# An encoder block on one core: value products of the attention with the values stationary in column halves, and group factors that are formed ahead of the values

## The chip, the cores and the metric

The kernel runs on one core of one Trainium2 chip. The metric is the device time of one execution in microseconds. The core has a tensor engine (PE, with its weight loads listed as PEld), a vector engine (DVE), a scalar engine (ACT), GpSimd (POOL) and a sync engine (SP); each works through its own list of instructions, whose order is fixed when the kernel is built, and waits on semaphores of the others. DMAs are issued by SP, POOL and ACT, and each of these engines issues them in the order of its own list.

## The reference, cut to what matters

One block of a hybrid encoder: a combined input projection, dilated window attention in three groups of four heads, gated linear attention (GLA), a gated merge of both, and an MLP. Sequence 1024, width 1024, all in float32. The part in question is the attention:

```python
outs, lses = [], []
for gi, (win, dil) in enumerate(ATTN_PAIRS):          # (128,1), (512,4), (2048,16)
    ...
    o_g, lse_g = _dilated_group(aq[:, :, hs], ak[:, :, hs], av[:, :, hs], bias, dil, k_side)
    outs.append(o_g)
    lses.append(lse_g)
mix_w = jax.nn.softmax(jnp.stack(lses, axis=0), axis=0)
y_attn = jnp.sum(mix_w[..., None] * jnp.stack(outs, axis=0), axis=0)
...
merged = (jax.nn.sigmoid(gate_a) * (y_attn @ w_attn_branch[l])
          + jax.nn.sigmoid(gate_g) * (y_gla @ w_gla_branch[l]))
```

Within a group, `m` is the maximum of a query's scores, `e = exp(s - m)`, `den = sum(e)`, the output `(e @ v) / den`, and `lse = m + log(den)`. The three groups' outputs of a head slot are so mixed with weights that come from the three pairs of `m` and `den`; the mix equals the sum of the three products `e @ v`, each with a factor per query and head (a share).

## The kernel before, in words

The projections are matmuls of 128x512 (`mm3`, L97, three passes L101 to L103 for each pair of split operands), cut into steps by `proj` (L588). Their results are collected in `cr`, a ring of four, and stored to the DRAM tile `spill` by SP (L621). The attention runs in between: 24 tiles of 128 queries, group g=2 first, then g=1, then g=0, eight tiles each. `att` (L762) makes the parts of a tile, and `visit` (L931) calls, for visit i, the loads of tile i+1, the values of tile i-2, the scores of tile i, the transposes of tile i-1, the blend of tile i-2 and the transposed mix of tile i-3. `units` (L942) spreads the visits over the projection steps. The tile scheduler that builds the program then settles the order on each engine, so that parts of neighbouring steps can trade places.

A tile's way: POOL loads q and k from `spill` (L770) and v from `vdr`; `scores` multiplies them on PE (L803, the two heads of a pair in the two row halves), DVE adds the bias and takes the maximum (L809, statistics in `sm`), ACT takes the exponential (L814); `turned` transposes `e` on PE (L830) and DVE and ACT copy it to `et` (L837). `values` (L844) multiplies: the stationary operand is `et` (128 keys x 128 queries), the moving one 64 columns of v, for each head; the result `avp` lies in one PSUM bank as 128 queries x 256. DVE copies it with the statistics into rows of 264 numbers (L854, L855). For g=2 and g=1 POOL stores those rows to `rows` in natural order; for g=0 POOL loads the rows of the other two groups back into `R` (L821), `weigh` (L878) and `blend` (L887) form factors and the mixed result on DVE and ACT, and `mixed` (L868) transposes it on PE (L872), copies it on ACT into `yat` and stores it to `yadr` by POOL (L874).

After the last projection steps `branches` loads the pieces of the GLA result (`ygdr`) and of the attention result (`yadr`) into `pre` by SP (L963), splits each in two on ACT and DVE (L148, L149) into `yg` and `ya`, and the merge multiplies them (`ps<-ya`, `ps<-yg`). SP's list also holds the branch weights (`raw<-in_wb`, L90) and the gates (`gate<-spill`, L1004).

## Time and profile before

| | |
|---|---|
| median of 3 runs | 1380.88 us (1380.69 to 1384.24) |
| profiled execution | 1383.76 us |
| its span, first to last instruction | 1382.0 us |
| mean granted TensorE clock | 0.997 |
| attention on PE (first scores to last values product) | 306.2 to 567.2 us |
| first merge matmul | 600.71 us |
| SP waiting at the spill stores for DVE's `cr` | 132.1 us |
| POOL waiting for `avp` before it loads v (L784) | 58.4 us |

The profile shows one execution; busy times of instructions overlap within an engine's pipeline, so that the distance between two starts is the price of the first. A row names the engine, the line, the operation and out<-in by the program's names. A DMA's row gives the median time from its issue to its landing.

### The profile page before, as it was taken

What the parts mean: (1) busy time and instruction counts of PE and PEld (TensorE: products, weight loads), DVE (VectorE), ACT (ScalarE), POOL (GpSimd) and SP (SyncE); (2) the same over time, 40 slices, a digit from 0 to 9 for tenths busy, and PEclk for the clock granted to TensorE, in tenths of its full rate; (3) what the DMA queues carried; (4) which work ended last, traced back from release to release, by engine and by line L of the source; (5) the groups of instructions that cost most, each with busy time, mean ns of one, the idle gap of its engine ahead of it and who ended that gap; (6) DMA issues with size and microseconds to landing.
All of it is one profiled execution on the core that took longest, in us unless ns stands there. A gap on an engine that the chain in (4) does not pass through costs nothing.

```text
span 1382.0 us, 19028 instructions
## 1 busy us (share of the span) xinstructions
PE 1370.8 (99%) x6837; PEld 1153.0 (83%) x6837; DVE 1011.3 (73%) x1748; ACT 630.7 (46%) x1207; POOL 99.1 (7%) x153
## 2 busy tenths in 40 slices
PE   9999999999999999999999999999999999999998
PEld 6989998788888888888888888888888888888886
DVE  6377768677565677666667787878867897786988
ACT  5346645334344344354416655555556433333343
POOL 0000100013222232000001000000000000000002
PEclk9999999999999999999999999999999999999998
DMA  7262326575444443465753565666655965445313
GB/s 247 71 190 87 108 71 225 183 206 176 157 145 159 136 143 127 139 225 191 270 213 141 200 221 191 222 208 217 219 205 157 365 220 167 152 131 160 105 31 122
DMA packets 105907, 238.57 MB, mean 173 GB/s; under 512 B 20101, under 2 KB 28805, under 8 KB 105812
## 3 DMA queue, kind: packets, MB, share of 16 engines
q1 hardware_dynamic: 99220, 218.47, 47.4%
q0 software_dynamic: 6304, 18.49, 4.4%
q8 instruction: 54, 0.88, 0.3%
q10 hardware_dynamic: 288, 0.39, 0.1%
q14 instruction: 41, 0.34, 0.1%
HBM read 160.67 MB, written 77.68 MB: 172 GB/s over the span
## 4 chain that ended last, share of the span: by engine, by line
PE 90%; DVE 3%; DMA 2%; issue 2%; ACT 2%; POOL 0%; SPq 0%; POOLq 0%; ACTq 0%; DVEq 0%
PE ps L101 18%; PE ps L102 18%; PE ps L103 18%; PE mm L101 9%; PE mm L102 9%; PE mm L103 9%; PE avp L844 2%; PE tr L830 1%; PE sc L803 1%; ACT xr L1196 1%; DMA xrh<-in_xT 1%; DMA praw<-in_wfm 1%; PE sc L406 0%; PE tr L376 0%; DMA pwhi<-in_wfm 0%
## 5 line engine op out<-in xcount | busy, mean ns | idle before, releaser
L1177 ACT CAST T<-hp 128x1024 fp32r<-128x1024 f32 x36 | 37.8, 1051 | 107.6 <-PE ps L102 68.1
L102 PE MATMUL mm<-wlo,x 128*128 128x272 f32 (+1 forms) x240 | 74.5, 311 | 0.7 <-DVE wlo L94 0.7
L101 PE MATMUL mm<-whi,x 128*128 128x272 f32 (+1 forms) x240 | 75.0, 313 | 0.0
L103 PE MATMUL mm<-whi,x 128*128 128x272 f32 (+1 forms) x240 | 74.6, 311 | 0.0
L814 ACT ACTIVATE e<-e,sm 128x256 f32<-128x256 f32 (+2 forms) x96 | 43.4, 453 | 51.6 <-DVE sm L809 51.6
L102 PE MATMUL ps<-B,B 128*128 128x512 f32 x160 | 62.2, 389 | 0.0
L103 PE MATMUL ps<-B,B 128*128 128x512 f32 x160 | 62.2, 389 | 0.0
L101 PE MATMUL ps<-B,B 128*128 128x512 f32 x160 | 60.9, 390 | 0.5 <-ACT B L1177 0.5
L101 PE MATMUL ps<-T,T 128*128 128x512 f32 x144 | 56.0, 389 | 0.0
L102 PE MATMUL ps<-B,T 128*128 128x512 f32 x144 | 56.0, 389 | 0.0
L102 PE MATMUL ps<-T,T 128*128 128x512 f32 x144 | 56.0, 389 | 0.0
L103 PE MATMUL ps<-B,T 128*128 128x512 f32 x144 | 56.0, 389 | 0.0
L103 PE MATMUL ps<-T,T 128*128 128x512 f32 x144 | 56.0, 389 | 0.0
L101 PE MATMUL ps<-B,T 128*128 128x512 f32 x144 | 56.0, 389 | 0.0
L1578 DVE TENSOR_TENSOR acc<-ps,acc 128x512 f32<-128x512 f32 x68 | 45.8, 690 | 12.8 <-PE ps L103 12.2
L1178 DVE TENSOR_TENSOR T<-hp,T 128x1024 fp32r<-128x1024 f32 x36 | 44.1, 1224 | 14.1 <-ACT T L1177 14.0
L101 PE MATMUL mm<-x,pwlo 128*128 128x512 f32 x128 | 51.1, 399 | 1.4 <-DVE cu L642 1.4
L642 DVE TENSOR_TENSOR cr<-cu,mm 128x512 f32<-128x512 f32 x44 | 35.2, 800 | 23.3 <-PE mm L103 23.0
L1683 POOL TENSOR_TENSOR mv<-mv,mhalf 128x1 f32<-128x1 f32 x8 | 7.0, 880 | 607.3 <-DVE mv L1682 605.8
L103 PE MATMUL mm<-x,pwlo 128*128 128x512 f32 x128 | 50.0, 391 | 0.0
L102 PE MATMUL mm<-x,pwlo 128*128 128x512 f32 x128 | 50.0, 391 | 0.0
L101 PE MATMUL ps<-T,fraw 128*128 128x512 f32 x128 | 49.6, 390 | 0.4 <-ACT T L1177 0.4
(497 smaller groups left out, 4228.8 us busy)
## 6 DMA issues: line engine op xcount, KB each, us to landing
hdr<-c SPq DMA_DIRECT2D x112, 256.0 KB, 2.5
hp<-hdr SPq DMA_DIRECT2D x56, 512.0 KB, 3.6
spill<-cr SPq DMA_DIRECT2D x64, 256.0 KB, 3.0
praw<-in_wfm SPq DMA_DIRECT2D x16, 512.0 KB, 5.0
pwhi<-in_wfm SPq DMA_DIRECT2D x16, 512.0 KB, 4.6
gate<-spill SPq DMA_DIRECT2D x32, 256.0 KB, 3.7
wa<-in_w SPq DMA_DIRECT2D x16, 512.0 KB, 4.5
wb<-in_w SPq DMA_DIRECT2D x16, 512.0 KB, 6.4
```

The lines of the kernel that those rows point to most:

```text
L101: T.matmul(ps, lh, rh, start=first and i == 0, stop=False, skip_group_check=more)
L102: T.matmul(ps, lh, rl, start=False, stop=False, skip_group_check=more)
L103: issued["pe"] = T.matmul(ps, ll, rh, start=False, stop=last and i == n - 1, skip_group_check=more)
L642: issued["add"] = V.tensor_tensor(o, a, b, op=OP.add)
L803: mm = T.matmul(sps[i][:, pr, 0:w], q[ps_, pr], k[ps_, pr, 0:w], start=True, stop=True)
L814: issued["exp"] = A.activation(e, e, AF.Exp, bias=sm[:, h:h + 1], scale=-1.0, accum_out=sm[:, 4 + h:5 + h])
L830: T.transpose(tp[0:hi - lo, pr, j], b["e"][i][:, pr, lo:hi], ident)
L844: return T.matmul(av[:, h * 64:h * 64 + 64], b["et"][h % 2][p0:p0 + vv.shape[0], h // 2, j], vv[:, h * 64:h * 64 + 64], start=j == h == 0, ...
L1177: A.copy(o[:, 0], src)
L1178: V.tensor_tensor(o[:, 1], src, o[:, 0].bitcast(F32), op=OP.subtract)
L1196: A.activation(q[i][:, k], tp[:, k], AF.Identity, bias=cols[:, c + 8:c + 9], scale=cols[:, c:c + 1])
L1578: V.tensor_tensor(m, p, m, op=OP.add)
```

## The change

The value products take v as the stationary operand, 64 columns at a time, and `et` (128 queries) as the moving one. The two heads of a pair write to the two column halves of the array, so that the result `avp` is already transposed: 64i.. partitions for the head's 64 values, two pairs, 128 queries. For g=2 and g=1 DVE copies it once and POOL stores it to `numdr`; the statistics go by themselves, as 8 numbers a query, to `smdr`, and `stats` loads them back for all eight tiles of g=0. For g=0 the factors are formed from the statistics alone in two units behind the scores (`weigh` with ACT's exponential, `shares`), transposed on PE into a third part of the same PSUM tile (`spread`, 12 x 128), copied by ACT to `fT` and stored by ACT to `fdr`. `loadw` reads them back with two SP DMAs into `W`, each line of 128 to 64 partitions; `quarter` loads the products of the other groups into `R` with four SP DMAs, for two tiles at a time. `values` then multiplies and adds on DVE in place in `W`, and POOL stores the result to `yadr` straight from there. The mix's transposes, `yat` and its ACT copies are gone. `W`, `fT` and `avp` are single buffers. The visits lose one round (26 for 27).

```diff
--- before.py
+++ after.py
@@ -110,7 +110,9 @@
     ygdr = dr.tile([4, 128, S], F32, name="ygdr")
     sdr = dr.tile([2, 5, 128, 2, 512], F32, name="sdr")
     yadr = dr.tile([2, 128, S], F32, name="yadr")
-    rows = dr.tile([2, S, 264], F32, name="rows")
+    numdr = dr.tile([2, 2, 128, S], F32, name="numdr")
+    smdr = dr.tile([2, S, 8], F32, name="smdr")
+    fdr = dr.tile([12, S], F32, name="fdr")
...
@@ -745,11 +747,12 @@
     kq_t, kk_t, kv_t = (ring(ap_, [128, 2, n], F32, m, nm) for nm, n, m in (("aq", 128, 3), ("ak", 256, 2), ("av", 256, 3)))
     e_t, et_t = (ring(ap_, [128, 2, 256], F32, m, nm) for nm, m in (("e", 4), ("et", 3)))
     sm_t, f_t = ring(ap_, [128, 8], F32, 3, "sm"), ring(ap_, [128, 5, 4], F32, 2, "f")
-    st_t, R_t = ring(ap_, [128, 264], F32, 2, "st"), ring(ap_, [128, 3, 264], F32, 2, "R")
+    R, W = ap_.tile([128, 2, 2, 256], F32, name="R"), ap_.tile([128, 3, 2, 128], F32, name="W")
+    s12, fT = ap_.tile([128, 8, 2, 8], F32, name="s12"), ap_.tile([12, 128], F32, name="fT")
+    st_t = turns([R[:, 1, i].rearrange("p (b n) -> p b n", b=2) for i in range(2)], 2)
     sc_t = turns([scp.tile([128, 2, 256], F32, tag="sc", name="sc") for _ in range(2)], 2)
     tr_t = turns([trp.tile([128, 2, 256], F32, tag="tr", name="tr") for _ in range(2)], 2)
-    av = avp.tile([128, 256], F32, tag="av", name="avp")
-    yat = ap_.tile([128, 2, 128], F32, name="yat")
+    av = avp.tile([128, 3, 128], F32, tag="av", name="avp")
 
...
@@ -815,10 +818,6 @@
                                                  accum_out=sm[:, 4 + h:5 + h])
 
         def turned():
-            if g == 0:
-                b["R"] = R_t()
-                for i in range(2):
-                    G.dma_start(b["R"][:, 1 + i], rows[i, t * 128:t * 128 + 128])
             b["et"] = []
             nb = len(b["blks"])
             for i in range(2):
@@ -840,9 +839,10 @@
             nb = len(b["blks"])
 
             def part(j, h):
+                i, pr = h % 2, h // 2
                 lo, hi, vv, p0 = b["blks"][j]
-                return T.matmul(av[:, h * 64:h * 64 + 64], b["et"][h % 2][p0:p0 + vv.shape[0], h // 2, j],
-                                vv[:, h * 64:h * 64 + 64], start=j == h == 0, stop=j == nb - 1,
+                return T.matmul(av[64 * i:64 * i + 64, pr], vv[:, h * 64:h * 64 + 64],
+                                b["et"][i][p0:p0 + vv.shape[0], pr, j], start=j == pr == 0, stop=j == nb - 1,
                                 skip_group_check=True)
 
             with tc.issue_after(part(0, 0).ins):
@@ -850,59 +850,82 @@
                     for h in range(4):
                         if j or h:
                             issued["small"] = part(j, h)
-            st = b["R"][:, 0] if g == 0 else st_t()
-            V.tensor_copy(st[:, 0:256], av)
-            V.tensor_copy(st[:, 256:264], b["sm"])
+            if g:
+                st = st_t()
+                V.tensor_copy(st, av[:, 0:2])
+                G.dma_start(numdr[g - 1, :, :, t * 128:t * 128 + 128].rearrange("b p n -> p b n"), st)
+                return
+            V.tensor_tensor(W[:, 0], av[:, 0:2], W[:, 0], op=OP.mult)
+            for i in range(2):
+                c = ORD[i + 1]
+                n = 128 // c
+                num = R[:, i].rearrange("p b (c j) -> p b j c", c=c)[:, :, t % 2 * n:t % 2 * n + n]
+                wn = W[:, i + 1].rearrange("p b (j c) -> p b j c", c=c)
+                for pr in range(2):
+                    V.tensor_tensor(wn[:, pr], num[:, pr], wn[:, pr], op=OP.mult)
+                V.tensor_tensor(W[:, 0], W[:, 0], W[:, i + 1], op=OP.add)
+            G.dma_start(yadr[:, :, t * 128:t * 128 + 128].rearrange("b p n -> p b n"), W[:, 0])
+
+        def weigh():
+            sm = b["sm"]
             if g == 1:
-                G.dma_start(rows[0].rearrange("(u j c) w -> c u j w", u=2, c=4)[t // 2, t % 2], st)
+                G.dma_start(smdr[0].rearrange("(u j c) w -> c u j w", u=2, c=4)[t // 2, t % 2], sm)
             elif g == 2:
-                G.dma_start(rows[1].rearrange("(j r) w -> r j w", r=8)[t], st)
+                G.dma_start(smdr[1].rearrange("(j r) w -> r j w", r=8)[t], sm)
             else:
-                b["f"] = weigh(b["R"])
-
-        def mix():
+                o = s12[:, t]
+                b["f"] = f = f_t()
...
+                A.activation(f[:, 0:3], f[:, 0:3], AF.Exp)
+
+        def shares():
             if g == 0:
-                b["o"] = o = st_t()[:, 0:256]
-                blend(b["R"], b["f"], o)
-
-        def mixed():
+                f, den, o = b["f"], b["sm"][:, 4:8], s12[:, t, :, 4:8]
+                V.tensor_tensor(den, den, f[:, 0], op=OP.mult)
+                V.tensor_tensor(o, o, f[:, 1:3], op=OP.mult)
+                V.tensor_tensor(f[:, 4], den, o[:, 0], op=OP.add)
+                V.tensor_tensor(f[:, 4], f[:, 4], o[:, 1], op=OP.add)
+                V.reciprocal(f[:, 4], f[:, 4])
+                V.tensor_tensor(f[:, 0:3], f[:, 0:3], f[:, 4:5].to_broadcast([128, 3, 4]), op=OP.mult)
+
+        def spread():
             if g == 0:
-                tp = tr_t()
-                for pr in range(2):
-                    T.transpose(tp[:, pr, 0:128], b["o"][:, pr * 128:pr * 128 + 128], ident)
-                A.copy(yat, tp[:, :, 0:128])
-                G.dma_start(yadr[:, :, t * 128:t * 128 + 128].rearrange("b p n -> p b n"), yat)
-
-        return load, scores, turned, values, mixed, mix
-
-    def weigh(R):
-        nm = R[:, :, 256:260]
-        f = f_t()
-        V.tensor_tensor(f[:, 3], nm[:, 0], nm[:, 1], op=OP.min)
-        V.tensor_tensor(f[:, 3], f[:, 3], nm[:, 2], op=OP.min)
-        V.tensor_tensor(f[:, 0:3], f[:, 3:4].to_broadcast([128, 3, 4]), nm, op=OP.subtract)
-        A.activation(f[:, 0:3], f[:, 0:3], AF.Exp)
-        return f
-
-    def blend(R, f, o):
-        den = R[:, :, 260:264]
-        V.tensor_tensor(den, den, f[:, 0:3], op=OP.mult)
-        V.tensor_tensor(f[:, 4], den[:, 0], den[:, 1], op=OP.add)
-        V.tensor_tensor(f[:, 4], f[:, 4], den[:, 2], op=OP.add)
-        V.reciprocal(f[:, 4], f[:, 4])
-        V.tensor_tensor(f[:, 0:3], f[:, 0:3], f[:, 4:5].to_broadcast([128, 3, 4]), op=OP.mult)
-        for g in range(3):
-            num = R[:, g, 0:256].rearrange("p (h d) -> p h d", h=4)
-            V.tensor_tensor(num, num, f[:, g].unsqueeze(2).to_broadcast([128, 4, 64]), op=OP.mult)
-        V.tensor_tensor(R[:, 0, 0:256], R[:, 0, 0:256], R[:, 1, 0:256], op=OP.add)
-        V.tensor_tensor(o, R[:, 0, 0:256], R[:, 2, 0:256], op=OP.add)
+                T.transpose(av[0:12, 2], b["f"][:, 0:3].rearrange("p g h -> p (g h)"), ident)
+                A.copy(fT, av[0:12, 2])
+                A.dma_start(fdr[:, t * 128:t * 128 + 128], fT)
+
+        def loadw():
+            if g == 0:
+                src = fdr.rearrange("(g b i) n -> i g b n", g=3, b=2)
+                for i in range(2):
+                    one = src[i, :, :, t * 128:t * 128 + 128]
+                    SP.dma_start(W[64 * i:64 * i + 64], one.unsqueeze(0).to_broadcast([64, 3, 2, 128]))
+
+        return load, scores, turned, values, weigh, shares, spread, loadw
+
+    def stats(g):
+        for u in range(2):
+            G.dma_start(s12[:, 4 * u:4 * u + 4, g - 1],
+                        smdr[g - 1, 512 * u:512 * u + 512].rearrange("(t p) w -> p t w", p=128))
+
+    def quarter(n):
+        u, q = n // 2, n % 2
+        for g in (1, 2):
+            c = ORD[g]
+            for pr in range(2):
+                src = numdr[g - 1, pr].rearrange("p (c u q j) -> p u q c j", c=c, u=2, q=2)[:, u, q]
+                dst = R[:, g - 1, pr].rearrange("p (c j) -> p c j", c=c)
+                SP.dma_start(dst, src)
 
     def flat(t):
         return t.rearrange("p a b -> p (a b)")[:, 0:512]
 
 
     gated = ap_.tile([128, 3, 512], F32, tag="strip1", name="gated")
-    gating = (turns([flat(e_t()) for _ in range(4)] + [flat(R_t()) for _ in range(2)], 6),
+    gating = (turns([flat(e_t()) for _ in range(4)] + [R[:, i].rearrange("p b n -> p (b n)") for i in range(2)], 6),
               turns([flat(et_t()) for _ in range(3)] + [gated[:, i] for i in range(3)], 6),
               turns([flat(kv_t()) for _ in range(3)], 3))
 
@@ -930,9 +953,11 @@
 
     def visit(i):
 
-        for n, part in ((i + 1, 0), (i - 2, 3), (i, 1), (i - 1, 2), (i - 2, 5), (i - 3, 4)):
+        for n, part in ((i + 1, 0), (i - 1, 6), (i - 2, 3), (i, 1), (i - 1, 2)):
             if 0 <= n < 24:
                 tiles[n][part]()
+        if i in (12, 16):
+            stats(2 if i == 12 else 1)
 
 
     n0 = len(steps) + 14
@@ -940,8 +965,14 @@
         steps += p["steps"]
     n1 = len(steps) - 7
     units = {}
-    for i in range(27):
-        units.setdefault(n0 + 1 + i * (n1 - n0) // 27, []).append(lambda i=i: visit(i))
+    for i in range(26):
+        n = n0 + 1 + i * (n1 - n0) // 27
+        units.setdefault(n, []).append(lambda i=i: visit(i))
+        for k, part, later in ((i, 4, 1), (i, 5, 2), (i - 1, 7, 1)):
+            if 0 <= k < 24 and (later == 1 or k > 15):
+                units.setdefault(n + later, []).append(lambda k=k, part=part: tiles[k][part]())
+        if i in (17, 19, 21, 23):
+            units[n + 1].append(lambda i=i: quarter((i - 17) // 2))
     for i in range(8):
 
         n = n0 - 18 + i * 3 // 2
```

The three places that follow show the end of the attention in the order of each engine. In the order of PE, ahead of the merge, `L844` is the values product, `L103`, `L101` are projection matmuls (`mm`), `L872` is the transposed mix. Before, the last product and what follows it:

```order
L103 MATMUL mm<-xT_2222,pwhi 128x512
L844 MATMUL avp<-av_2253,et_2259 128x64
L844 MATMUL avp<-av_2253,et_2260 128x64
...
L872 MATMUL tr<-ident,st_2266 128x128 x2
L101 MATMUL mm<-x_91,pwlo 128x512
L102 MATMUL mm<-x_91,pwlo 128x512
L103 MATMUL mm<-x_91,pwlo 128x512
```

Behind it stand 144 projection matmuls and then the first `ps<-ya`. In the changed program, from the last projection matmul on (`L896` is the transposed set of factors, `L829` the transposes of `e`, `ps<-yg` the merge):

```order
L103 MATMUL mm<-x_94,px 128x512
L896 MATMUL avp<-ident,f_2267 12x128
L844 MATMUL avp<-et_2262,av_2254 64x128
L844 MATMUL avp<-et_2260,av_2254 64x128
...
L829 MATMUL tr<-ident,e_2258 128x128 x4
L829 MATMUL tr<-ident,e_2259 128x128 x4
L844 MATMUL avp<-et_2261,av_2255 64x128
L844 MATMUL avp<-et_2262,av_2255 64x128
...
L101 MATMUL ps_5183<-yg_5002,whi 128x512
L101 MATMUL ps_5176<-yg_5002,whi 128x512
```

The products of tiles 22 and 23 have moved behind all projection matmuls, and the merge begins with `yg` in place of `ya`. Between the product of tile 21 and the last projection matmul stand one block of scores, one of transposes and 24 projection matmuls.

SP's list at the same place, before (`pre` are the merge's pieces, `raw` its weights):

```order
L621 DMA spill<-cr_2105 128x512
L963 DMA pre<-ygdr 128x512 x4
L963 DMA pre<-yadr 128x512
L621 DMA spill<-cr_2106 128x512
L963 DMA pre<-yadr 128x512
L621 DMA spill<-cr_2107 128x512
L621 DMA spill<-cr_2108 128x512
L963 DMA pre<-yadr 128x512 x2
L90 DMA raw<-in_wb 128x768
L963 DMA pre<-ygdr 128x512
```

And in the changed program:

```order
L905 DMA W<-fdr 64x6x128 x2
L90 DMA raw<-in_wb 128x768
L623 DMA spill<-cr_2110 128x512
L1035 DMA gate<-spill 128x512 x9
L905 DMA W<-fdr 64x6x128 x2
L994 DMA pre<-ygdr 128x512 x4
L994 DMA pre<-yadr 128x512 x4
L994 DMA pre<-ygdr 128x512 x4
L1035 DMA gate<-spill 128x512
```

The pieces have moved from among the spill stores to behind the last one and behind the factors of the last two tiles; nine gates have moved ahead of them.

DVE's list at the end of the attention, in the changed program (`L865` are the products of the other groups with their factors, `L858` that of the tile itself, `L866` the additions, `L836` the copy of the transposes, `L151` the split of the pieces):

```order
L865 TENSOR_TENSOR W<-R,W 128x128 x4
L858 TENSOR_TENSOR W<-avp,W 128x256
L836 COPY et_2261<-tr 128x512
L866 TENSOR_TENSOR W<-W 128x256 x2
L858 TENSOR_TENSOR W<-avp,W 128x256
L865 TENSOR_TENSOR W<-R,W 128x128 x4
L866 TENSOR_TENSOR W<-W 128x256 x2
L151 TENSOR_TENSOR yg_5002<-pre,yg_5002 128x512 x4
L151 TENSOR_TENSOR ya_4998<-pre,ya_4998 128x512
```

Before, the corresponding rows of the last tile stand among projection work:

```order
L854 COPY R_2269<-avp 128x256
L896 TENSOR_TENSOR R_2269<-R_2269,f_2265 128x256
L897 TENSOR_TENSOR R_2269<-R_2269 128x256
L898 TENSOR_TENSOR st_2267<-R_2269 128x256
L149 TENSOR_TENSOR pwlo<-pwhi,pwlo 128x512
L642 TENSOR_TENSOR cr_2106<-cu_2103,mm 128x512
```

The copy of the transposes that the last product needs now stands behind the multiplication of tile 22, and the splits of the pieces follow the last addition directly.

4 lines of the change are left out of this document (added).

## The prediction

> **What bounds the kernel now.** I read the head of the page first, then the chain that ended last, then the stage that the change touches by windows, and only then single rows.
>
> ```profile
> PE 1370.8 (99%) x6837; PEld 1153.0 (83%) x6837; DVE 1011.3 (73%) x1748; ACT 630.7 (46%) x1207; POOL 99.1 (7%) x153
> PE 90%; DVE 3%; DMA 2%; issue 2%; ACT 2%; POOL 0%; SPq 0%; POOLq 0%; ACTq 0%; DVEq 0%
> 530.00:560.00 30.00, 30.00 (x173) 25.43 (x172) 25.80 (x79) 12.95 (x36) 4.88 (x8) 1.00 0.40 122
> 560.00:575.00 15.00, 15.00 (x77) 12.59 (x76) 6.92 (x13) 4.58 (x9) 1.47 (x2) 1.00 0.38 117
> 575.00:610.00 35.00, 35.00 (x155) 28.83 (x154) 20.19 (x31) 15.19 (x24) 0.72 (x1) 1.00 0.66 220
> ```
>
> TensorE (PE) is busy 99% of the span and holds 90% of the chain. In the windows (columns after the stretch: sum, then PE, PEld, DVE, ACT, POOL) it is full through the end of attention and the start of the merge. So a microsecond of PE work taken out here shortens the kernel, and a microsecond in which PE stands still lengthens it; work of DVE, ACT, POOL or the queues counts only where PE comes to wait for it.
>
> The prices of PE's work come from its timeline (start, busy time, line):
>
> ```profile
> 540.47 0.38 PE L872 MATMUL tr<-ident,st 128*128 128x128 f32 x2
> 540.68 0.78 PE L844 MATMUL avp<-av,et 128*128 128x64 f32 x6
> 541.27 0.48 PE L101 MATMUL mm<-x,pwlo 128*128 128x512 f32 x1
> ...
> 544.12 1.22 PE L844 MATMUL avp<-av,et 128*128 128x64 f32 x10
> 545.27 0.92 PE L803 MATMUL sc<-ak,aq 64*128 64x192 f32 x8
> 546.13 1.09 PE L830 MATMUL tr<-ident,e 128*128 128x128 f32 x8
> 546.98 0.47 PE L103 MATMUL mm<-xT,pwhi 128*128 128x512 f32 x1
> ...
> 565.48 2.03 PE L844 MATMUL avp<-av,et 128*128 128x64 f32 x16
> 567.44 0.44 PE L872 MATMUL tr<-ident,st 128*128 128x128 f32 x2
> 567.64 0.48 PE L101 MATMUL mm<-x,pwlo 128*128 128x512 f32 x1
> ...
> 600.71 0.39 PE L101 MATMUL ps<-ya,whi 128*128 128x512 f32 x1
> ```
>
> I take differences of starts, since busy times overlap. One tile's values product is 16 passes: 10 in 1.15 and 6 in 0.59 us, so 0.109 each. A transpose pass over 128 columns costs 0.85 / 8 = 0.106, or 0.83 ns a column. Eight score passes over 192 columns, whose row halves stand in different halves of the array, take 0.86; one after another at 0.83 ns a column they would take 1.27. So **halves of the array do run at once** in this trace, for rows. Between 567.64 and 600.71 stand the 144 projection matmuls that the old order puts behind the last values product: 33.07 / 144 = 0.23 us each. They cover everything that happens between that product and the merge.
>
> **The change, part by part.**
>
> *Values on PE.* There are 320 passes at L844 (160 products). With 64 stationary columns and 128 moving ones, two heads can share the array. At once: 160 pairs; a pair cannot beat one pass over 128 columns (0.106), so 0.109 and 17.4 us in place of 34.9, **−17.4**. One after another: 320 passes at the same 0.109, so nothing. A middle case is set by the weight loads:
>
> ```profile
> L366 PEld LDWEIGHTS tr<-ident,k x32: 139/141/143, 80.0 to 177.4; 128*128 128x128 f32 x32
> L316 PEld LDWEIGHTS tr<-ident,lr x8: 124/126/128, 54.4 to 58.1; 128*96 128x96 f32 x8
> L830 PEld LDWEIGHTS tr<-ident,e x160: 108/140/198, 312.4 to 557.9; 128*128 128x128 f32 x140, 128*64 128x64 f32 x20
> ```
>
> 128, 96 and 64 columns load in 141, 126 and (the minimum) 108 ns. If only these 33 ns come off a 0.109 load and loads stay serial, a pair takes 0.15 and the product saves 34.9 − 160 × 0.152 = 10.6. I take −17.4, being nearest to the score row, the only one of two halves; the ends are −17.4 and 0.
>
> *A rule weighed.* The 10 value passes ahead of L803 take 1.15, and 10 at 0.106 would be 1.06: 0.09 us stands where the row layout changes, and the sum has it already on both sides. The Trainium skill, "TensorEngine Tiling (Array Packing)", Key Properties, says that changing the tiling mode drains the TensorE, and that tiles work independently. By the first, 24 products and 8 narrow transposes, entered and left, would each meet a drain; by the second the halves run at once, as the score row shows for rows. Rival 4 prices the first from the row.
>
> *Transposes.* 16 passes (L872) go, 0.21 / 2 = 0.105 each; 8 small ones of the factors come. 8 × 0.106 − 16 × 0.105 = −0.8. PE's work: **−18.2**.
>
> *Other engines outside the tail.* DVE's prices are these:
>
> ```profile
> L897 DVE TENSOR_TENSOR R<-R x8: 417/422/427, 486.9 to 568.5; 128x256 f32<-128x256 f32 x8
> L891 DVE TENSOR_TENSOR f<-f,R x8: 159/161/164, 471.0 to 554.7; 128x4 f32<-128x4 f32 x8
> L809 DVE CUSTOM_DVE_ANT_0 e<-sc,strip x96: 270/354/426, 306.9 to 548.3; 128x256 f32<-128x256 f32 x40, 128x128 f32<-128x128 f32 x32, 128x192 f32<-128x192 f32 x24
> L809 DVE DVE_READ_ACCUMULATOR2_ANT sm<- x96: 70/84/93, 307.1 to 548.6; 128x1 f32 x96
> L837 DVE COPY et<-tr x19: 407/684/690, 313.7 to 558.7; 128x512 f32<-128x512 f32 x11, 128x256 f32<-128x256 f32 x8
> ```
>
> A g=0 tile loses a 128x256 copy, three multiplications, two additions and a small copy (6 × 0.42 + 0.16 = 2.7) and gets one multiplication of 128x256, four of 128x128 (between 0.16 and 0.42, I take 0.28), two additions and two small operations (2.7). DVE stays as full as it was, beside PE. POOL stores and loads as many pieces as before, at 7% busy. SP gets 32 more issues, 0.32 us each (row below), 10 us over some 100 us. ACT trades eight copies of 128x256 for eight of 12x128 and eight issues. All of this lies beside PE as long as a g=0 visit is long: the new order has 60 to 84 projection matmuls in one, 14 to 19 us, and a tile's new round trip (DVE 3.7, store 3.1, load 3.2) is 10.0. The spill stores queued behind the loads of W have a ring of four buffers as cover; without it each visit would add up to the 3.1 of a store.
>
> *The tail.* This is the price. In the new order only 24 projection matmuls, one score block and two blocks of transposes stand behind the product of tile 21, and none behind that of tile 23; the merge follows directly, with the GLA pieces first. And pre<-ygdr, which the old order had far ahead, is queued on SP behind the last W<-fdr, which waits for W, a single buffer. Its rows:
>
> ```profile
> yadr<-yat POOLq DMA_DIRECT2D x8, 128.0 KB, 3.1
> pre<-yadr SPq DMA_DIRECT2D x4, 256.0 KB, 3.1
> pre<-ygdr SPq DMA_DIRECT2D x8, 256.0 KB, 4.0
> R<-rows POOLq DMA_DIRECT2D x16, 132.0 KB, 2.5
> aq<-spill POOLq DMA_DIRECT2D x24, 128.0 KB, 3.8
> tdr<-trow SPq DMA_DIRECT2D x12, 256.0 KB, 7.2
> DMA to landing us min/median/max: 2.2/3.1/4.6
> L963 SPq DMA_DIRECT2D pre<-ygdr x8: 319/382/407, 572.0 to 593.8; - x8
> L148 ACT CAST yg<-pre x8: 620/622/627, 582.3 to 600.0; 128x512 fp32r<-128x512 f32 x8
> ```
>
> (The line of minimum, median and maximum is that of the tile yat, so of the store yadr<-yat.) The load of W is not in this trace: 192 KB in 512-byte pieces, lying between R<-rows at 2.5 and aq<-spill at 3.8; a broadcast store, tdr<-trow, took 7.2. I take 3.2, the ends are 2.5 and 7.2. From the end V of tile 21's product:
> - DVE: multiplication 0.42, four score reductions 4 × (0.354 + 0.084), copy of et 0.68, two additions 0.84: V + 3.7.
> - Store of yadr 3.1, load of W for tile 22 3.2: V + 10.0.
> - DVE: 4 × 0.28 + 0.42 + copy 0.68 + 0.84 = 3.1; store 3.1: V + 16.2.
> - SP issues two W (0.64), then pre<-ygdr 4.0, ACT's cast 0.62: first merge matmul at **V + 21.4**.
> - PE's work until then: scores 0.86, transposes 2 × 0.85, 24 × 0.23, two products 2 × 0.87, the small transpose 0.1: 9.9. PE stands still for **11.5**.
> - W for tile 23 lands at 16.2 + 3.2, DVE 2.4, store 3.1, pre<-yadr 3.1, cast 0.62: ya is there at V + 28.6. PE has 10 GLA matmuls, 2.3, until V + 23.7: another **4.9**.
>
> Together +16.4.
>
> *The clock.* The granted clock (second figure from the right but two) falls where PE is left idle at the very end:
>
> ```profile
> 1360.00:1370.00 10.00, 10.00 (x46) 8.28 (x45) 9.05 (x23) 4.54 (x12) 1.84 (x2) 1.00 0.29 107
> 1376.00:1382.00 6.00, 1.22 (x2) 0.50 (x2) 0.84 (x2) 1.17 (x3) 0.00 (x0) 0.50 0.49 176
> ```
>
> It is 1.00 with PE full and 0.50 with PE busy for 1.22 of 6 us. A stall of 11.5 us would find it at half as well, and the matmuls behind it run slower until it is back; how long no row shows. Between nothing and 3 us (half speed through a stretch of 6 us), I take +1. The Trainium skill, "TensorE: Matmul & The Clock Gate", on the HAM clock gate, gives about 3.4 us of sustained work until the full clock is back, by which the loss is an estimated 1.7 per long stall; the fall agrees with the row above, the return is shown by no run here.
>
> *Sum:* −18.2 + 16.4 + 1 = −0.8 on the profiled execution, 1383.76 us (span 1382.0, the rest lies around it): 1383.0. The median of the three runs is 1380.88, 2.9 below it, and the same step from there is **1380**.
>
> **The rivals.**
>
> 1. *The tail is shorter.* If the stores land at their minimum of 2.2 and the loads of W at 2.5, three stores and two loads take 0.9 × 3 + 0.7 × 2 = 4.1 out of the chain, and the sum is −5: 1376; with pre<-yadr at 2.5 too, and no clock loss, 1374. For: the queues are quieter in the tail, with no projection weights left to fetch. Against: gate<-spill loads stand there now, nine just ahead on SP.
> 2. *The column halves do not run at once* (ends slower). No row has two column halves; if the array takes them one after another, −18.2 becomes −0.8 and the stall, with 1.7 us more work on PE ahead of it, 14.7: **+15, 1396**. It makes the kernel slower by over 0.3% from a pair price of about 0.15 on, where the gain is 10.6 and the sum +5. For: only row halves are seen at once. Against: nothing in the score rows depends on which halves they are.
> 3. *W lands late* (ends slower). A load of W as dear as tdr<-trow's 7.2 adds 4.0 twice to the chain; at aq<-spill's 3.8 and stores of 3.8 it is 0.6 × 2 + 0.7 × 3 = 3.3. That gives +3 to +7: 1383 to 1388. For: it reads the same six lines 64 times over. Against: 7.2 was measured when 16 projection weights were in flight.
> 4. *A change of layout costs time every time* (ends slower). 24 products and 8 narrow transposes, entered and left, at the 0.09 us that stands between L844 and L803: 64 × 0.09 = 5.8, sum +5, 1386. Against: a transpose of 64 columns between those of 128 has no longer passes (the median of all 160 is 273 ns, the minimum 272):
>
> ```profile
> L830 PE MATMUL tr<-ident,e x160: 272/273/331, 312.4 to 558.0; 128*128 128x128 f32 x140, 128*64 128x128 f32 x20
> ```
>
> 5. *The change does not do what it says*: PE, not the queue, is late at the merge, and no stall appears. Then the whole −18 stays: 1363. The order on each engine is fixed, so I give this little.
>
> **How the numbers follow.** A time within 0.3%, 4.1 us either way, is about what a measurement of this kernel can tell from no change. Forecast, halves at once and the gain given back in the tail: 0.45, 1377 to 1385. Shorter tail: 0.18, and 0.05 for rival 5, together 0.23 faster. Halves not at once 0.16, W late 0.11, layout changes 0.05: together 0.32 slower. The predicted time is 1380. The range runs from rival 1's lower end to rival 2's time, 1374 to 1396; it leaves out rival 5 and mixtures beyond rival 2.
>
> **What would show it.** Right: L844's passes start in pairs, with some 0.109 a pair; PE full until the last projection matmul; then a gap of about 11 us ahead of the first ps<-yg, ended by pre<-ygdr, and a second of about 5 ahead of ps<-ya, ended by pre<-yadr; SP waiting at the last W<-fdr. Wrong: L844's stretch as long as before (rival 2), a gap below 8 us in all (rivals 1 and 5), PE gaps inside the g=0 visits (the spill ring fails as cover), or W<-fdr landing beyond 4 us (rival 3).

## The result, and the profile after

| kernel | median of four runs, us (lowest to highest) | against before (95% interval) | span of the profiled run, us | clock |
|---|---|---|---|---|
| before | 1380.79 (1379.21 to 1384.24) | | 1382.0 | 0.997 |
| changed | 1418.04 (1413.81 to 1419.26) | 1.0261 (1.0231 to 1.029) | 1417.1 | 0.983 |

The change makes the kernel 37 us slower; the forecast was 1380, the range 1374 to 1396. The profiled execution of the kernel before is one of its longer ones, so the spans differ by 35.1 only. The head of the page and the windows of the changed kernel (stretch: sum, PE, PEld, DVE, ACT, POOL busy with counts; then granted clock, DMA share, GB/s):

```profile
PE 1370.2 (97%) x6829; PEld 1136.3 (80%) x6829; DVE 1008.4 (71%) x1748; ACT 631.8 (45%) x1207; POOL 105.3 (7%) x157
480.00:530.00 50.00, 44.52 (x222) 34.59 (x221) 31.94 (x102) 18.96 (x53) 6.54 (x9) 0.95 0.43 133
530.00:560.00 30.00, 30.00 (x166) 23.86 (x165) 19.44 (x58) 9.60 (x26) 4.85 (x7) 0.96 0.46 144
560.00:575.00 15.00, 11.49 (x63) 8.97 (x61) 7.12 (x23) 5.03 (x13) 0.24 (x1) 1.00 0.40 103
575.00:600.00 25.00, 20.91 (x112) 16.28 (x107) 15.95 (x52) 9.35 (x26) 1.86 (x3) 0.86 0.52 140
600.00:620.00 20.00, 8.09 (x58) 5.96 (x56) 6.10 (x19) 6.10 (x10) 1.47 (x2) 0.77 0.57 177
620.00:640.00 20.00, 7.84 (x20) 5.38 (x21) 6.01 (x14) 6.27 (x11) 0.73 (x1) 0.55 0.53 163
```

PE is no longer full from 480 us on, and the clock is below 1.00 in most of the same stretches. The stalls of PE of more than 0.3 us from there on stand in its timeline (start, busy time, last the idle time ahead and what ended it):

```profile
484.57 0.79 PE L101 MATMUL mm<-xT,pwlo 128*128 128x512 f32 x1 [2.21 <-ACT cr L669]
529.41 0.79 PE L101 MATMUL mm<-xT,pwhi 128*128 128x512 f32 x1 [3.20 <-DVE cr L644]
571.39 0.27 PE L896 MATMUL avp<-ident,f 128*12 128x128 f32 x1 [3.35 <-DVE f L892]
591.18 0.38 PE L896 MATMUL avp<-ident,f 128*12 128x128 f32 x1 [4.09 <-DVE f L892]
604.15 1.09 PE L844 MATMUL avp<-et,av 128*64 128x128 f32 x16 [0.34 <-ACT fT L897]
614.66 2.17 PE L844 MATMUL avp<-et,av 128*64 128x128 f32 x16 [8.40 <-DVE et L836]
631.84 1.47 PE L101 MATMUL ps<-yg,whi 128*128 128x512 f32 x2 [15.01 <-ACT yg L150]
```

The first four, 12.9 us, lie inside the g=0 visits, the last three, 23.8 us, where the merge should begin. Behind most of them is one transfer, as the experiments below show; it stands in the list of DMAs and in the waits of DVE:

```profile
W<-fdr SPq DMA_DIRECT2D x16, 192.0 KB, 7.9
pre<-ygdr SPq DMA_DIRECT2D x8, 256.0 KB, 7.0
DVE W L865 <- DMA W<-fdr: 46.4, 7, 8.1
DVE W L858 <- DMA W<-fdr: 15.2, 1, 15.2
```

The load of W takes 7.9 us, not 3.2, and DVE waits 61.6 us for it. That median rests on the three loads of 16 for which the profile gives a landing; by the semaphore records in the trace all 16 landed after 6.3 to 9.4 us. The clock is at half in four stretches (columns: sum, PE's busy time and count, clock, DMA share, GB/s):

```profile
484.47:487.88 3.41, 3.31 (x8) 0.50 0.22 81
528.85:532.26 3.41, 2.85 (x7) 0.50 0.50 144
590.29:597.12 6.83, 5.94 (x31) 0.50 0.58 118
610.77:638.08 27.31, 8.11 (x29) 0.50 0.58 184
```

The account between the two profiled executions is then: stalls from 260 us on 38.0 in place of 2.2, +35.8; the 320 passes of the value products (summed over the distances of their starts in the trace) 24.7 in place of 36.1, -11.4; transposes 0.5 in place of 1.5, -1.0; the lower clock, half of the 20.21 us that PE was busy in those stretches, an estimated +10.1. The sum is +33.5, and 1417.1 - 1382.0 is 35.1. The rest is not in these rows: a change of layout ahead of each product (e4_swap_alone below) would add some 2.4, and some of the value passes ran at half clock and are counted twice.

### The profile page after: what moved, and what is told of

Its sections match the earlier page's. It is cut to its first block, busy times and chain, and to the rows that moved or that the text cites. A ratio compares the mean times of both kernels' runs of the same rounds, so it can differ in the third digit from the quotient of the medians.

```text
span 1417.1 us, 19085 instructions
## 1 busy us (share of the span) xinstructions
PE 1370.2 (97%) x6829; PEld 1136.3 (80%) x6829; DVE 1008.4 (71%) x1748; ACT 631.8 (45%) x1207; POOL 105.3 (7%) x157
## 4 chain that ended last, share of the span: by engine, by line
PE 54%; DMA 2%; ACT 1%; DVE 0%; issue 0%; SPq 0%; DVEq 0%; ACTq 0%
PE ps L102 18%; PE ps L101 18%; PE ps L103 18%; DMA W<-fdr 1%; ACT xr L1227 1%; DMA yadr<-W 0%; DMA gate<-spill 0%; PE ps L1224 0%; PE ps L1735 0%; PE ps L1731 0%; ACT T L1208 0%; PE avp L844 0%; ACT B L1208 0%; PE sc L806 0%; PE mm L103 0%
## 5 line engine op out<-in xcount | busy, mean ns | idle before, releaser
L101 PE MATMUL mm<-whi,x 128*128 128x272 f32 (+1 forms) x240 | 75.1, 313 | 0.0
L103 PE MATMUL mm<-whi,x 128*128 128x272 f32 (+1 forms) x240 | 74.6, 311 | 0.0
L103 PE MATMUL ps<-B,B 128*128 128x512 f32 x160 | 62.2, 389 | 0.0
L101 PE MATMUL ps<-B,B 128*128 128x512 f32 x160 | 60.9, 390 | 0.5 <-ACT B L1208 0.5
L101 PE MATMUL ps<-T,T 128*128 128x512 f32 x144 | 56.0, 389 | 0.0
L103 PE MATMUL ps<-T,T 128*128 128x512 f32 x144 | 56.0, 389 | 0.0
L101 PE MATMUL ps<-B,T 128*128 128x512 f32 x144 | 56.0, 389 | 0.0
L103 PE MATMUL ps<-B,T 128*128 128x512 f32 x144 | 56.0, 389 | 0.0
L644 DVE TENSOR_TENSOR cr<-cu,mm 128x512 f32<-128x512 f32 x44 | 35.3, 802 | 28.5 <-PE mm L103 27.7
L101 PE MATMUL mm<-x,pwlo 128*128 128x512 f32 x128 | 50.6, 395 | 1.0 <-DVE cu L644 1.0
L101 PE MATMUL mm<-xT,pwhi 128*128 128x512 f32 x120 | 48.1, 401 | 3.2 <-DVE cr L644 3.2
L103 PE MATMUL mm<-x,pwlo 128*128 128x512 f32 x128 | 50.3, 393 | 0.0
```

Source lines behind the costliest of these rows:

```text
L101: T.matmul(ps, lh, rh, start=first and i == 0, stop=False, skip_group_check=more)
L103: issued["pe"] = T.matmul(ps, ll, rh, start=False, stop=last and i == n - 1, skip_group_check=more)
L644: issued["add"] = V.tensor_tensor(o, a, b, op=OP.add)
```

## The experiments

Twelve kernels, grouped by question; times are medians, ratios are those to the kernel before on the same chip.

**W from different lines (e1_own_lines).** A line is here a stretch of DRAM that is read in one piece, 512 bytes for the load of W. On the changed kernel, the load reads other numbers from another DRAM tile:

```diff
-                src = fdr.rearrange("(g b i) n -> i g b n", g=3, b=2)
+                src = spill[24:30].rearrange("(g b) p n -> p g b n", g=3)
                 for i in range(2):
-                    one = src[i, :, :, t * 128:t * 128 + 128]
-                    SP.dma_start(W[64 * i:64 * i + 64], one.unsqueeze(0).to_broadcast([64, 3, 2, 128]))
+                    SP.dma_start(W[64 * i:64 * i + 64], src[64 * i:64 * i + 64, :, :, t * 128:t * 128 + 128])
```

> W is loaded from 64 different lines of another DRAM tile in place of the same line 64 times; pieces (512 bytes), size (192 KB), wait for W and place in SP's list stay, the factors that the output is mixed with are other numbers. Theory 1 (the load of W is dear because it reads the same lines 64 times): the load lands in 3 to 4 us instead of 8, the four stalls of PE inside the g=0 visits (12.9 us) go, the tail's stall falls from 23.7 to about 16, the clock loss falls by some 8: 1418 - 13 - 8 - 8 = about 1389 us (1380 to 1395). Rival (the chain over the single buffer W and the place of the loads in SP's list cost the time, whatever a load takes): over 1410 us.

1386.61 us, ratio 1.0044 (1.0028 to 1.006). The list of its DMAs:

```profile
W<-spill SPq DMA_DIRECT2D x16, 192.0 KB, 3.8
pre<-ygdr SPq DMA_DIRECT2D x8, 256.0 KB, 4.6
```

The same number of pieces of the same size, from 64 different lines, lands in 3.8 us, the pieces of the merge behind it land in 4.6 again, and 31 of the 37 us are gone. No stall is left inside the visits. This is what theory 1 said. By the semaphore records, the 14 loads beside the g=0 tiles landed after 3.4 to 4.3 us; the two of the first tile are issued earlier, in another stretch. The trace's packets show where the time goes: a piece takes 27 ns in the median in both kernels, but in the first 1.5 us from the first piece on 122 to 178 pieces of a tile's two loads begin in the changed kernel, and 529 to 667 here. Two other things have changed with the lines: the load no longer waits for the store of the factors (the first one is issued at 356.5 us in place of 470.1), and its access no longer has a step of zero from one partition to the next. The first is answered by e8a_long_lines below, which keeps the wait; the second isn't told apart from the lines.

**The multiplications held back on DVE (e2_mults_behind).**

```diff
-            V.tensor_tensor(W[:, 0], av[:, 0:2], W[:, 0], op=OP.mult)
+            first = V.tensor_tensor(W[:, 0], av[:, 0:2], W[:, 0], op=OP.mult)
...
-                    V.tensor_tensor(wn[:, pr], num[:, pr], wn[:, pr], op=OP.mult)
+                    with tc.issue_after(first.ins):
+                        V.tensor_tensor(wn[:, pr], num[:, pr], wn[:, pr], op=OP.mult)
```

> The changed kernel with the four multiplications R x W of a tile held back until its own product with W is issued, so that DVE reaches the wait for W later in its list. Theory (DVE stands at the wait for W ahead of projection work that PE waits for): the stalls inside the visits (12.9 us, and some 5 of clock) shrink by more than half, the tail stays: about 1405 us. Rival (PE waits for W whatever DVE's order is): no change, 1418 us.

1409.92 us, 1.0212 (1.0188 to 1.0236): 8 us better, where 13 were expected; with two runs, 1407.19 and 1412.66, its interval just overlaps that of the changed kernel. In the changed kernel DVE's timeline shows the reason for the edit, and that of this run why it gives so little:

```profile
526.81 0.37 DVE L865 TENSOR_TENSOR W<-R,W 128x128 f32<-128x128 f32 x1 [5.22 <-DMA W<-fdr]
...
528.67 0.68 DVE L644 TENSOR_TENSOR cr<-cu,mm 128x512 f32<-128x512 f32 x1
```

```profile
528.06 0.69 DVE L637 TENSOR_TENSOR pwhi<-pwhi 128x512 f32<-128x512 f32 x1 [9.39 <-DMA pwhi<-in_wfm]
528.67 0.68 DVE L644 TENSOR_TENSOR cu<-cu,mm 128x512 f32<-128x512 f32 x1
```

SP's timeline of this run, at the same place:

```profile
514.44 1.28 SPq L906 DMA_DIRECT2D W<-fdr  x2
515.82 0.56 SPq L610 DMA_DIRECT2D pwhi<-in_wfm  x1
```

In the changed kernel DVE stands 5.22 us at the wait for W, and the addition that frees PE's bank (L644) comes behind; PE's stall of 3.20 ends there. With the wait out of the way DVE waits for projection weights instead: they were issued right behind the two loads of W and came 12 us later, where such a load takes 4.9 in the median of that run. So, as far as these rows show, a load of W also holds up what is queued behind it, and DVE's order is only part of the matter. What the edit shows is mixed: the stalls up to the product of tile 21 fall from 12.9 to 7.9 us, those behind it stay (25.1 against 23.8), and the edit also moved the 24 projection matmuls that stood behind that product ahead of it.

**The swap by itself (e4_swap_alone).** On the kernel before:

```diff
-                return T.matmul(av[:, h * 64:h * 64 + 64], b["et"][h % 2][p0:p0 + vv.shape[0], h // 2, j],
-                                vv[:, h * 64:h * 64 + 64], start=j == h == 0, stop=j == nb - 1,
+                i, pr = h % 2, h // 2
+                return T.matmul(av[64 * i:64 * i + 64, pr * 128:pr * 128 + 128], vv[:, h * 64:h * 64 + 64],
+                                b["et"][i][p0:p0 + vv.shape[0], pr, j], start=j == pr == 0, stop=j == nb - 1,
```

> The kernel before with one edit: v is the stationary operand in column halves, everything behind it as before; the result lies transposed where the rest takes it as not transposed, so the mix is of other numbers. Theory (the halves run at once, a pass in the mean 0.077 us instead of 0.113 as the traces of before and after have it): 36.1 - 24.7 = 11.4 us off PE at no cost elsewhere: 1369 us. Rival (the gain is taken back by waits for v or avp): 1376 to 1381 us.

1370.48 us, 0.9928 (0.9913 to 0.9942). PE has no stall between 300 and 600 us; a tile's product and its neighbours in the timeline:

```profile
543.38 0.38 PE L873 MATMUL tr<-ident,st 128*128 128x128 f32 x2
543.69 1.09 PE L845 MATMUL avp<-et,av 128*64 128x128 f32 x16
544.72 0.55 PE L830 MATMUL tr<-ident,e 128*128 128x128 f32 x3
```

The product takes 1.03 us. Eight pairs of 0.109 would be 0.87: 0.16 is the change of the layout on leaving. Two transposes ahead of it take 0.31 to its start, and 0.21 in the kernel before: another 0.10 on entering. 24 products at 0.26 are 6.2 us. The 0.16 is part of the passes' own sum, which is 24.0 us in this run, 12.1 below the kernel before; the 0.10 stands in the rows ahead, and 24 of them, 2.4, come off that gain. What is left, 9.7, is what the medians show: 1380.27 - 1370.48 = 9.8. (The 24.0 are 6.6 above the 17.4 of the prediction, more than 24 x 0.16 = 3.8: some products are split into pieces, and each piece pays.)

**Which halves (e5_same_half, e12_one_half).** The first only orders the heads otherwise, `for h in (0, 2, 1, 3)`. The second:

```diff
-                return T.matmul(av[64 * i:64 * i + 64, pr * 128:pr * 128 + 128], vv[:, h * 64:h * 64 + 64],
+                return T.matmul(av[0:64, h * 128:h * 128 + 128], vv[:, h * 64:h * 64 + 64],
...
-            V.tensor_copy(st[:, 0:256], av)
+            for i in range(2):
+                V.tensor_copy(st[64 * i:64 * i + 64, 0:256], av[0:64, 256 * i:256 * i + 256])
```

> As e4_swap_alone (the kernel before with v stationary in column halves, the mix of other numbers), but the four heads of a block in the order 0, 2, 1, 3, so that most neighbours use the same column half. Theory (a pass runs beside the one ahead of it only if that one is in the other half): of four products in a row only the middle two overlap, three steps of 0.107 a pass in place of two, values up by at least 8 us against e4_swap_alone: 1378 to 1386 us. Rival (the array takes any two 64-column passes together, or the gain comes from shorter weight loads alone): 1369 to 1372 us as e4_swap_alone.

> As e4_swap_alone (the kernel before with v stationary, the mix of other numbers), but all four heads write to the same column half, partitions 0 to 63 of the bank; DVE copies it in two pieces of 64 partitions. Theory 2a (a pass is short because its weight load has 64 columns in place of 128, whichever half it is in): 16 passes still take some 0.9 us and the time is that of e4_swap_alone, 1370 us (1369 to 1374, DVE has 24 more copies of 0.4 us). Theory 2b (two passes overlap only in different halves, as the prediction had it): each pass takes 0.107, values are back at 34 us or more, 1380 us or more.

e5_same_half took 1371.79 us (0.9936, 0.9916 to 0.9955), e12_one_half 1388.59 (1.0056, 1.0039 to 1.0073). Their timelines, a product and the row behind it, of the first and of the second:

```profile
544.79 1.14 PE L845 MATMUL avp<-et,av 128*64 128x128 f32 x16
545.87 0.66 PE L830 MATMUL tr<-ident,e 128*128 128x128 f32 x4
```

```profile
548.95 1.52 PE L845 MATMUL avp<-et,av 128*64 128x128 f32 x12
550.41 0.91 PE L803 MATMUL sc<-ak,aq 64*128 64x192 f32 x7
```

In one half, 12 passes take 1.46 us, 0.109 each and the layout change; over both halves in either order 16 take about 1.05. So **the two column halves do run at once, and the gain of the swap is all of that**: in one half the kernel is slower than before, since the layout changes come on top. The expectation for e5_same_half was wrong: the order of the heads matters by 0.05 us a product, 1.2 in all (the medians differ by 1.3, within their intervals), so PE overlaps passes that are not next to each other in its list. There a product has four passes of one half ahead of the first of the other; how much farther ahead it looks wasn't tried.

**The factors without DMA (e6_pe_spread).** DVE widens the factors into W, PE transposes six blocks, ACT copies back:

```diff
-                T.transpose(av[0:12, 2], b["f"][:, 0:3].rearrange("p g h -> p (g h)"), ident)
-                A.copy(fT, av[0:12, 2])
-                A.dma_start(fdr[:, t * 128:t * 128 + 128], fT)
...
+                V.tensor_copy(W.rearrange("p g b (i d) -> p (g b i) d", i=2),
+                              f[:, 0:3].rearrange("p g h -> p (g h)").unsqueeze(2).to_broadcast([128, 12, 64]))
+                tp = tr_t().rearrange("p g (b n) -> p g b n", b=2)
+                for n in range(3):
+                    for pr in range(2):
+                        T.transpose(tp[:, n - 1, pr] if n else av[:, 2 + pr], W[:, n, pr], ident)
+                A.copy(W[:, 0], av[:, 2:4])
+                A.copy(W[:, 1:3], tp)
```

> The changed kernel without fT, fdr and the loads of W: DVE writes each factor 64 times beside each other into W, PE transposes six blocks of 128x128 into PSUM, ACT copies them back to W. Theory (the DMA round trip of the factors is what costs): PE gets 48 - 8 more transposes, 40 x 0.107 = 4.3 us, DVE some 8 x 1 us beside PE, values 11.4 less, old transposes 1.5 less, and 36 projection matmuls (8 us) now stand behind the last product, so that at most 10 us of stall remain at the merge: between 1370 and 1384 us. Rival (DVE and ACT, with three more operations in the chain of a tile, hold PE up inside the visits): over 1390 us.

1378.36 us, 0.9984 (0.9975 to 0.9994). The 48 transposes cost PE 4.5 us, the stall at the merge is 2.5, and none lies inside the visits. Without the round trip the change is no loss.

**Long lines, and copies of them (e8a_long_lines, e8b_eight_copies).** The first lays the six lines of a half behind each other:

```diff
-    fdr = dr.tile([12, S], F32, name="fdr")
+    fdr = dr.tile([2, 8, 1, 6, 128], F32, name="fdr")
...
-                A.dma_start(fdr[:, t * 128:t * 128 + 128], fT)
+                A.dma_start(fdr[:, t, 0].rearrange("i q n -> q i n"), fT)
...
-                    SP.dma_start(W[64 * i:64 * i + 64], one.unsqueeze(0).to_broadcast([64, 3, 2, 128]))
+                    one = fdr[i, t].rearrange("c q n -> c (q n)")
+                    SP.dma_start(W[64 * i:64 * i + 64].rearrange("p g b n -> p (g b n)"),
+                                 one.unsqueeze(1).to_broadcast([1, 64, 768]))
```

The second has eight in place of 1 in the tile's third place, eight ACT writes and reads of eight partitions from each copy.

> The changed kernel with the factors laid out in DRAM so that a half of W for one tile is one line of 3 KB, still read 64 times by one load: 64 pieces of 3 KB in place of 384 of 512 bytes, same bytes. Theory 1a (the load is slow by the number of small reads of the same line): it lands in 3 to 4.5 us and the time is about that of e1_own_lines, 1382 to 1392 us. Theory 1b (slow by the bytes that are read from the same place): it lands in 6 to 8 us as before and the time stays at 1405 to 1420 us.

> As e8a_long_lines, with eight copies of each 3 KB line, written by eight DMAs of ACT a tile, each read 8 times. Theory 1b: the copies spread the reads, the load lands in 3 to 4.5 us where e8a_long_lines needs 6 to 8. Theory 1a: no difference in the landing between the two. ACT has 56 more issues of 0.3 us, 17 us beside PE, which may delay a tile's factors by 2 us.

e8a_long_lines: 1386.26 us, 1.004 (1.0025 to 1.0055); e8b_eight_copies: 1412.29, 1.0229 (1.0208 to 1.0249). DMAs and PE's stalls of the first, and ACT's issues of the second:

```profile
W<-fdr SPq DMA_DIRECT2D x16, 192.0 KB, 3.6
pre<-ygdr SPq DMA_DIRECT2D x8, 256.0 KB, 4.4
...
582.35 1.09 PE L844 MATMUL avp<-et,av 128*64 128x128 f32 x16 [0.34 <-ACT fT L897]
588.27 1.86 PE L844 MATMUL avp<-et,av 128*64 128x128 f32 x16 [3.80 <-DVE et L836]
599.84 0.80 PE L101 MATMUL ps<-yg,whi 128*128 128x512 f32 x1 [9.71 <-ACT yg L150]
```

```profile
L899 ACTq DMA_DIRECT2D fdr<-fT x64: 706/714/1302, 467.0 to 617.4; - x64
```

Still one line read 64 times, the same bytes, and the load lands in 3.6 us (3.1 to 4.7 by the semaphore records): it is the 384 small reads of the same lines that are slow, not the bytes from one place. This load waits for the store of the factors as that of the changed kernel does, so that e1_own_lines did not gain by losing that wait. The kernel's time is that of e1_own_lines. The eight copies can't be read cleanly: ACT spends 64 x 0.71 = 46 us on issues, 0.71 each where I had reckoned with 0.3, and the factors come late. The profile gives no median landing for that load. By the packets in the trace the two loads of a tile take 4.0 to 6.5 us from the first issue to the last piece, and 3.3 to 4.8 in e8a_long_lines: no sign that copies help a long line, in a kernel whose queues are not alike.

**More cover at the merge (e10, e14, e16, e17).** One number, on e6_pe_spread, e8a_long_lines and the changed kernel:

```diff
-        n = n0 + 1 + i * (n1 - n0) // 27
+        n = n0 + 1 + i * (n1 - n0) // 35
```

(31 in e10_earlier_visits), and e17_long_early_behind adds the edit of e2_mults_behind to e14_long_lines_early.

> As e6_pe_spread, with the 26 visits spread over 26/31 instead of 26/27 of the projection steps: 104 projection matmuls (24 us) stand behind the last product instead of 36. Theory (what is left of the tail costs e6_pe_spread its 2.5 us gap and a slow start of the merge of about 2): 1374 us (1371 to 1377). Rival (shorter visits make PE wait inside them for DVE's chain of a tile): 1378 us or more.

> As e8a_long_lines (3 KB lines of factors), with the 26 visits spread over 26/35 of the projection steps in place of 26/27: 48 projection matmuls (11 us) stand behind the last product. Theory (what is left of the loss in e8a_long_lines, 13.5 us of stall and some 4 of clock at the merge, is missing cover): the stall at the merge falls below 3 us, 1386 - 12 - 4 = 1370 us (1367 to 1376). Rival (the shorter visits are too short for a tile's round trip, or the chain over the single W ends no earlier): 1380 us or more.

> The changed kernel (W read as 384 pieces of 512 bytes) with the visits spread as in e14_long_lines_early. Theory (cover alone does not mend it: the load of W takes 8 us in each visit, visits are now shorter, and DVE stands at the wait for W): stalls inside the g=0 visits of over 13 us remain and the time stays over 1400 us. Rival (cover at the merge was all that was missing): below 1385 us.

> As e14_long_lines_early, with the multiplications R x W held back until the tile's own product is issued (the edit of e2_mults_behind). Theory (the 3.7 us of stall that e14_long_lines_early still has inside the visits come from DVE standing at the wait for W ahead of projection work): they fall below 1.5 us, with 36 instead of 48 projection matmuls behind the last product the stall at the merge stays at 1 to 3 us: 1371 to 1375 us. Rival (they come from weights that land late behind the loads of W in SP's list): no change, 1376 us or more.

| run | median, us | ratio (95% interval) | stalls from 300 us on, us: up to the last product, behind it |
|---|---|---|---|
| e10_earlier_visits | 1374.38 | 0.9958 (0.9941 to 0.9974) | 0, 0.8 |
| e14_long_lines_early | 1375.93 | 0.9965 (0.9953 to 0.9977) | 3.7, 1.7 |
| e16_changed_early | 1413.46 | 1.0238 (1.0217 to 1.0258) | 23.9, 7.3 |
| e17_long_early_behind | 1378.25 | 0.9981 (0.9972 to 0.9991) | 0, 9.1 |

In e10, e14 and e16 the stall behind the last product lies ahead of projection matmuls, and the merge itself begins without one; in e17 it lies at the merge. With the load at its usual price, cover takes the rest: e14_long_lines_early is 10 us below e8a_long_lines (the expectation had 16). With the slow load cover alone moves the stalls into the visits, which are now shorter (e16). In e17 the stalls inside the visits do go, as its theory said; but with 36 matmuls behind the last product the merge stalls for 9.1, where 1 to 3 were expected, and the time misses the expected 1371 to 1375. Why that stall is so much longer than in e14 is open. e10_earlier_visits and e14_long_lines_early, whose mix is that of the reference, are 0.4% below the kernel before; their intervals overlap, so neither is the faster.

## Why the prediction was wrong, point by point

- **"Halves of the array do run at once"**: right, shown for columns by e12_one_half.
- **Values -17.4**: mis-sized, -11.4 in the passes' own sum and some 9 to 10 with the changes of layout ahead of them (9.8 by the medians of e4_swap_alone). The pair does cost 0.109, but each product meets a change of layout on both sides, 0.26 us by e4_swap_alone. That was rival 4's mechanism; it gave 5.8 in all, the runs show 6.2. The Trainium skill, "TensorEngine Tiling (Array Packing)", Key Properties, says that a change of the tiling mode drains the TensorE: these runs agree, with 0.26 us for the two changes around a product. It had a chance of 0.05 because I took the transposes of 64 columns, whose passes are not longer, as evidence against it. They carry the label 128*64 as the new products do; what tells the two apart wasn't tried.
- **"I take 3.2" for a load of W**: the step that failed. I chose between R<-rows (2.5) and aq<-spill (3.8), which read different lines, and set aside tdr<-trow (7.2), the one row of the trace that, like the new load, reads a line over and over, with the argument that it was measured beside 16 weight loads. The load took 7.9; e1_own_lines and e8a_long_lines together show that it takes both, repeated lines and small pieces. That 7.2 would have been so near is in part luck: tdr<-trow writes DRAM to DRAM from a line of 2 KB, and a load that read lines of 3 KB over and over took 3.6; what makes tdr<-trow slow wasn't tried.
- **Rival 3, at 7.2, +7**: the right mechanism with a price five times too small. It put the longer load into the tail's chain only. Three things were missing. First, the cover inside the visits: a round trip of 3.7 + 3.1 + 7.9 = 14.7 us fills a visit of 14 to 19, and DVE's multiplications with W stand in its list ahead of the additions that free PE's banks and of the factors `f` that PE transposes, so that DVE's wait becomes PE's (two stalls ended by `cr`, two by `f`, 12.9 us). Second, what is queued behind the load comes late too: pre<-ygdr took 7.0 in place of 4.0, by the semaphore records 7.7 to 9.4 for the four pieces right behind the loads of W, which take 3.5 to 4.4 in e1_own_lines, and 4.1 to 5.2 for the four after them.
- The third is **the clock, "+1"**: it cost an estimated 10.1 us, as a loss in four stretches instead of one at the merge. The first of the four windows above follows the stall of 2.21 us: half the clock for 3.41 us, 1.7 us lost. The Trainium skill, "TensorE: Matmul & The Clock Gate", HAM clock gate, gives some 3.4 us of sustained work until the full clock is back; this trace agrees behind the first two stalls (from the end of the stall 3.3 and 2.9 us), and it took 5.9 us behind that of 4.09 and 6.2 behind that of 15.01.
- **The tail**: the mechanism as predicted. The chain of the changed kernel, in order of time (start, length, step; steps under 0.1 us are left out):

```profile
600.09 2.24 DMA yadr<-W
602.35 8.11 DMA W<-fdr
610.48 5.08 DMA gate<-spill
615.56 0.24 issue
615.80 4.75 DMA yadr<-W
620.61 0.58 SPq L905
621.24 9.25 DMA W<-fdr
```

  Store, load of W, store, SP's last loads of W, with pre<-ygdr behind them. (The row that names a gate's load is put down to the wrong transfer: in that stretch the second half of W lands and DVE works, as its timeline shows.)

```profile
612.47 1.21 DVE L865 TENSOR_TENSOR W<-R,W 128x128 f32<-128x128 f32 x4 [8.05 <-DMA W<-fdr]
```

  From the end of tile 21's product (595.5) to the first merge matmul (631.84) it is 36.3 us where 21.4 were predicted. With the load at 3.6, in e8a_long_lines, the three stalls are 0.34 + 3.80 + 9.71 = 13.9 where the prediction had 11.5 ahead of the merge and 16.4 in all. The total is near it by two misses that cancel in part: the way to the merge is longer, 25.4 from the product of tile 21 (574.5) to the first merge matmul for 21.4, and the 4.9 ahead of ya is 0.2. In the changed kernel the stall ahead of ya did not appear either: the last load of W had landed by the time the late yg did.
- **Other engines cost nothing outside the tail**: right in e1_own_lines and e8a_long_lines, which have no stall inside the visits; wrong in the changed kernel, by the load of W.

Put together for e8a_long_lines, where the load has its usual price: passes 23.5 in place of 36.1, -12.6; transposes -1.0; stalls from 260 us on 14.3 in place of 2.2, +12.1; clock, half of the 7.08 us that PE is busy in the one stretch at half clock (588.64 to 605.71), an estimated +3.5; 24 changes of layout ahead of the products, +2.4. The sum is +4.4; the spans differ by 1385.4 - 1382.0 = 3.4 and the medians by 1386.26 - 1380.65 = 5.6. So the change was no gain even at the price that I had assumed for the load.

## What to carry to other kernels

Price a transfer by the row whose access is alike, not by the one of like size: here many small reads of the same few lines cost twice what the same reads of different lines did, and what was queued behind them came late. Where no row is alike in both, pieces and lines, the price is a range, and its dear end belongs in every place where the transfer is waited for. Before calling a round trip hidden, look at what stands behind its wait in the waiting engine's own list. And when a producer moves towards its consumer, give the last round trip work to lie beside; one number in the spread of the visits was worth 4 us on e6_pe_spread and 10 on e8a_long_lines.

## What the runs showed of the hardware that was not expected

- A load of 192 KB as 384 pieces of 512 bytes from six lines read 64 times: 7.9 us; from 64 different lines: 3.8; as 64 pieces of 3 KB from one line: 3.6. The single piece of 512 bytes is no slower (27 ns in the median in both cases), the pieces begin at a lower rate; why is not settled.
- A stall of PE of 2.21 us was followed by half the granted clock for 3.41 us, but a longer one need not be: after the stall of 3.35 us that ends at 571.39 the clock was 1.00 (and behind the stall of 2.01 us in e6_pe_spread too).

```profile
564.00:571.30 7.30, 4.04 (x18) 1.00 0.32 90
571.30:575.00 3.70, 3.45 (x27) 1.00 0.20 72
```

- Passes in different column halves overlap even where two products of the same half stand next to each other in PE's list (1.08 us against 1.03 for 16).
- An ACT issue of the 6 KB store took 0.71 us with the line split in two halves (e8b_eight_copies), and 0.30 without in the changed kernel:

```profile
L898 ACTq DMA_DIRECT2D fdr<-fT x8: 296/297/557, 468.6 to 604.2; - x8
```
